# MoBA scores on halves of the TensorE array: each head's products on its own 64 rows, each head into its own PSUM bank

## The chip, the cores and the metric

The kernel runs on one NeuronCore of a Trainium2 chip. The metric is the device time of one execution in microseconds (us). TensorE (PE) multiplies, VectorE (DVE) and ScalarE (ACT) read its results from PSUM and do the elementwise work, GpSimd (POOL) works on SBUF only, and SyncE (SP) issues the DMAs. All engines run beside each other and wait for one another by semaphores; each works off its own instructions in the order in which the program lists them.

## The reference, cut to what matters

The program is a decoder trunk of four layers over 256 tokens of width 1024. Layers 0 and 3 mix tokens by native sparse attention (NSA), layer 1 by MoBA, layer 2 by a short convolution; each layer ends with a SwiGLU feed-forward part. The change is in the one MoBA layer. With 256 tokens there is one MoBA block, so no past block is selected and the layer is plain causal attention with 16 heads of width 64:

```python
q, k, v = jnp.split(h @ w_in, 3, axis=-1)
q = heads(q) * (HEAD_DIM ** -0.5)
k = heads(k); v = heads(v)
m_own = own_pos[None, :] <= tq[:, None]
s_own = jnp.einsum('bhqd,bhkd->bhqk', qc, k_own)
p = masked_softmax(s_own, m_own)
o = jnp.einsum('bhqk,bhkd->bhqd', p.astype(v_own.dtype), v_own)
return o @ w_out
```

## The kernel before, in words

All large products are made from float32 values that are split into a high part (rounded to float32r, the format in which TensorE takes them in one instruction) and a low part (the rest). A product of two such values is three matmuls: high by high, high by low, low by high. Weights come from memory in parts of 128 x 1024; the high part is a CAST on ACT or DVE (line 109) and the low part a subtraction on DVE or POOL (line 110). Five buffers hold the high parts and five the low parts (`W_BUFS`), so the CAST of a later part can only start when TensorE is done with the part that had the buffer.

In the MoBA layer two heads are worked on together, as a pair: there are eight pairs, called p0 to p7 here. `MOBA_ORDER` lists the steps of the layer: `V` values, `k` a projection of the keys of one pair, `q` a projection of its queries, `s` its scores and softmax, `T` the transposes of its probabilities, `P` their product with the values. A projection is 24 matmuls (lines 128 to 130) into one PSUM bank of the pool "A"; DVE then scales the result (line 324), and ACT and DVE split it (lines 166 and 167 for queries, 379 and 380 for keys). The pool "A" has four banks, "B" three and "C" one. They are handed out in turn: who asks for a fifth bank of "A" waits until the last reader of the first one is done.

The two heads of a pair lie in the 128 partitions: head 0 in partitions 0 to 63, head 1 in 64 to 127. The keys are kept in a tile `keys` of 128 partitions with one half for each head, and the 64 partitions that belong to the other head hold zeros (`pad_keys`). So `scores` (line 412) can use all 128 partitions: for the first 128 tokens (t = 0) three matmuls of 256 columns (two heads by 128 keys) fill one bank, and for the other 128 tokens (t = 1) three matmuls of 512 columns (two heads by 256 keys) fill another. Half of what is multiplied is zero.

`softmax` (line 345) then does, for each of four blocks (t = 0 head 0, t = 0 head 1, t = 1 head 0, t = 1 head 1), one instruction on DVE that adds the mask and takes the row's extreme (line 354, with a second short instruction that reads the extreme out), one exponential on ACT (line 357), and after a reciprocal of the four sums on DVE (line 359) one multiplication on POOL (line 361). `turn` transposes the result on TensorE into banks of "B" (lines 431 to 434) and splits it into tiles `pt` (lines 166 and 167); `weigh` multiplies by the values into the bank of "C" and splits the outcome (lines 453 and 454).

The program's instructions are written in the order of the steps, and a scheduler at build time then sets the order on each engine; it knows nothing of the measured times. So an edit of one step can move instructions of others.

Of the kernel before, what the change touches and what calls it, by code (L numbers as in the profile page):

```python
# [16 lines left out]
P = 128  # L17
D = 1024
S = 256
# [4 lines left out]
DH = 64  # L24
# [27 lines left out]
class Kernel:  # L52
# [334 lines left out]
    def moba(self, norm):  # L387
        nc, at = self.nc, self.begin(norm)
        mm = nc.tensor.matmul
# [21 lines left out]

        def scores(p):
            q, kt = qs[p], self.keys[p % 4]
            s = []
            for t in range(NT):
                n = (t + 1) * P
                o = self.bank("A")[:, :2 * n].rearrange("p (a s) -> p a s", a=2)
                c = slice(t * P, (t + 1) * P)
                mm(o, q[:, 0, c], kt[:, 0, :, :n], start=True, stop=False)
                mm(o, q[:, 1, c], kt[:, 0, :, :n], start=False, stop=False)  # L420
                mm(o, q[:, 0, c], kt[:, 1, :, :n], start=False, stop=True)
                s.append(o)
            cols = [(s[t][:, i], slice((t + i) * S if t else i * P, (t + i + 1) * S if t else (i + 1) * P))
                    for t in range(NT) for i in range(2)]
            prs.append(self.softmax(cols, [1.0] * 4))

# [14 lines left out]
        def weigh(p):  # L441
# [8 lines left out]
            for i in range(2):  # L450
# [5 lines left out]

        self.steps(MOBA_ORDER, {"V": lambda _: self.values(at, put_values), "k": project_k, "q": project_q,
                                "s": scores, "T": turn, "P": weigh})
        self.out_proj(outs, norm + 1)

# [483 lines left out]
```

## Time and profile before

| | |
|---|---|
| median of three runs | 1308.08 us (1306.71 to 1308.45) |
| the profiled execution | 1307.79 us |
| its span, from the first to the last instruction | 1306.0 us |
| busy in the span: PE / DVE / ACT / POOL | 1259.8 / 985.9 / 715.6 / 319.9 us |
| mean granted clock of TensorE | 0.993 |
| the chain of work that ended last, by engine | PE 84%, DVE 9%, the rest 2% or less each |
| the MoBA scores | eight pairs, first matmul at 402.2 us, last at 456.7 us |

The span is what the trace covers; the 1.8 us around it belong to the execution too. Busy time of PE counts an instruction until its result has left the array, so instructions overlap in the trace: how fast PE works is read from the distance of their starts, not from their durations.

### The profile page before, as it was taken

To read this page: it belongs to the slowest core of one execution; us is meant where nothing else is said; L and a number is where in the kernel's file an instruction comes from. 1 tells how busy PE (TensorE), PEld (TensorE's weight loads), DVE (VectorE), ACT (ScalarE), POOL (GpSimd) and SP (SyncE) were. 2 spreads that over 40 slices of the span, in tenths; PEclk is the share of its full clock that TensorE was granted. 3 is DMA by queue.
4 is the path that set the end of the run, shared out by engine and by line. 5 is a ranking of instruction groups with operands and counts; after the bars stand their busy time and mean duration, and the time that the engine had idled before them with its cause. 6 is when DMAs were issued, how large, how long until landed. Compare 5 with 4: busy or idle time off the path is not lost.

```text
span 1306.0 us, 21378 instructions
## 1 busy us (share of the span) xinstructions
PE 1259.8 (96%) x7820; PEld 1122.1 (86%) x7820; DVE 985.9 (75%) x1939; ACT 715.6 (55%) x1443; POOL 319.9 (24%) x346
## 2 busy tenths in 40 slices
PE   6988999999999899999999999999998989999997
PEld 6977788888889888888899988888898878888886
DVE  6688899775778888876667789765767797997753
ACT  3468857564434546655433447564324797666532
POOL 5557620000247220000113120000244765000011
PEclk9999999999999999999999999999999999999999
DMA  6623065656554335755565655656555312565551
GB/s 231 244 86 102 17 208 163 209 184 197 185 172 149 100 114 179 212 189 194 165 201 170 200 179 171 201 186 195 189 179 193 98 49 66 193 210 187 187 179 60
DMA packets 60728, 215.24 MB, mean 165 GB/s; under 512 B 7248, under 2 KB 7632, under 8 KB 60624
## 3 DMA queue, kind: packets, MB, share of 16 engines
q1 hardware_dynamic: 60480, 213.85, 50.5%
q8 instruction: 61, 1.00, 0.3%
q14 instruction: 43, 0.35, 0.1%
q10 hardware_dynamic: 144, 0.04, 0.0%
HBM read 212.81 MB, written 1.05 MB: 164 GB/s over the span
## 4 chain that ended last, share of the span: by engine, by line
PE 84%; DVE 9%; ACT 2%; issue 2%; POOL 2%; DMA 1%; POOLq 0%; DVEq 0%; ACTq 0%
PE psA L148 30%; PE psA L152 15%; PE psB L148 11%; PE psB L152 5%; PE psA L130 4%; PE psA L128 4%; PE psA L129 4%; PE psB L549 2%; DVE pt L167 1%; DVE pr L354 1%; ACT pr L357 1%; DVE ff L167 1%; PE psA L337 1%; POOL wlo L110 1%; DVE wlo L110 1%
## 5 line engine op out<-in xcount | busy, mean ns | idle before, releaser
L109 ACT CAST whi<-raw 128x1024 fp32r<-128x1024 f32 (+1 forms) x354 | 369.0, 1043 | 297.4 <-PE psB L148 110.6
L110 DVE TENSOR_TENSOR wlo<-raw,whi 128x1024 fp32r<-128x1024 f32 (+1 forms) x334 | 412.4, 1238 | 140.1 <-ACT whi L109 134.9
L148 PE MATMUL psA<-ff,whi 128*128 128x512 f32 x840 | 231.2, 396 | 0.2
L148 PEld LDWEIGHTS psA<-ff,whi 128*128 128x128 f32 x840 | 149.0, 188 | 25.1 <-DVE ff L167 0.6
L195 POOL TENSOR_TENSOR ssq<-ssq,row 128x256 f32<-128x256 f32 x54 | 50.7, 938 | 483.4 <-issue 291.5
L148 PE MATMUL psA<-pt,whi 128*128 128x512 f32 x640 | 166.4, 395 | 0.0
L128 PE MATMUL psA<-at,whi 128*128 128x256 f32 x552 | 160.5, 291 | 5.9 <-ACT whi L109 5.9
L130 PE MATMUL psA<-at,wlo 128*128 128x256 f32 x552 | 159.0, 289 | 3.8 <-DVE wlo L110 3.8
L129 PE MATMUL psA<-at,whi 128*128 128x256 f32 x552 | 159.1, 288 | 0.0
L110 POOL TENSOR_TENSOR wlo<-raw,whi 128x1024 fp32r<-128x1024 f32 (+1 forms) x56 | 132.4, 2370 | 82.1 <-ACT whi L109 52.5
L148 PEld LDWEIGHTS psA<-pt,whi 128*128 128x128 f32 x640 | 116.5, 188 | 21.2
L152 PEld LDWEIGHTS psA<-ff,wlo 128*128 128x128 f32 x840 | 122.8, 188 | 12.4
L152 PE MATMUL psA<-ff,wlo 128*128 128x256 f32 x840 | 129.2, 281 | 0.0
L128 PEld LDWEIGHTS psA<-at,whi 128*128 128x128 f32 x552 | 108.5, 197 | 6.2 <-ACT whi L109 5.9
L130 PEld LDWEIGHTS psA<-at,wlo 128*128 128x128 f32 x552 | 108.2, 196 | 4.4 <-DVE wlo L110 4.4
L129 PEld LDWEIGHTS psA<-at,whi 128*128 128x128 f32 x552 | 108.6, 197 | 0.5
L152 PEld LDWEIGHTS psA<-pt,wlo 128*128 128x128 f32 x640 | 87.1, 188 | 7.3
L152 PE MATMUL psA<-pt,wlo 128*128 128x256 f32 x640 | 88.9, 281 | 0.0
L148 PE MATMUL psB<-pt,whi 128*128 128x512 f32 x320 | 84.8, 395 | 0.0
L361 POOL TENSOR_SCALAR pr<-pr,rc,gates 128x256 f32<-128x256 f32 (+1 forms) x128 | 70.3, 563 | 38.6 <-DVE rc L359 32.5
L357 ACT ACTIVATE pr<-pr,mn 128x128 f32<-128x128 f32 (+1 forms) x160 | 71.3, 449 | 9.5 <-DVE mn L354 8.7
L292 ACT ACTIVATE row<-gu 128x256 f32<-128x256 f32 x88 | 36.8, 418 | 67.9 <-DVE gu L284 61.2
(207 smaller groups left out, 2210.6 us busy)
## 6 DMA issues: line engine op xcount, KB each, us to landing
raw<-in_w SPq DMA_DIRECT2D x384, 512.0 KB, 4.0
wf<-in_w SPq DMA_DIRECT2D x16, 512.0 KB, 4.4
h<-in_xt SPq DMA_DIRECT2D x4, 256.0 KB, 5.4
raw<-in_w SPq DMA_DIRECT2D x4, 256.0 KB, 5.4
out<-ff SPq DMA_DIRECT2D x4, 256.0 KB, 2.5
w<-in_w SPq DMA_DIRECT2D x2, 256.0 KB, 3.8
mask<-in_mask SPq DMA_DIRECT2D x1, 128.0 KB, 6.6
cneg<-in_cneg SPq DMA_DIRECT2D x1, 128.0 KB, 6.3
```

The costliest lines, as they stand in the source:

```text
L109: copy(hi[:, c], src[:, c])
L110: eng.tensor_tensor(out=lo[:, c], in0=src[:, c], in1=hi[:, c].bitcast(F32), op=OP.subtract)
L128: mm(out, wt[0], act[0], start=first, stop=False)
L129: mm(out, wt[0], act[1], start=False, stop=False)
L130: mm(out, wt[1], act[0], start=False, stop=last)
L148: mm(outs[o], w[0], acts[k].rearrange("p i s -> p (i s)"), start=(k == 0), stop=(k == n - 1))
L152: mm(outs[o][:, :S], w[1], acts[k][:, 0, :], start=False, stop=False)
L167: self.nc.vector.tensor_tensor(out=dst[:, 1], in0=src, in1=dst[:, 0].bitcast(F32), op=OP.subtract)
L195: nc.gpsimd.tensor_tensor(out=self.ssq, in0=self.ssq, in1=sq, op=OP.add)
L292: nc.scalar.activation(sg, gu[:, 0, :], AF.Silu)
L357: nc.scalar.activation(pr[:, c], pr[:, c], AF.Exp, bias=mn[:, j:j + 1], scale=-1.0, accum_out=den[:, j:j + 1])
L361: nc.gpsimd.tensor_scalar(pr[:, c], pr[:, c], rc[:, j:j + 1], gates[j], op0=OP.mult, op1=OP.mult)
```

## The change

`scores` takes its two banks at the start, one for each head instead of one for each half of the tokens. Each matmul takes 64 partitions of queries and keys (those of one head), and the two heads alternate. Per pair there are twelve matmuls in place of six: for t = 0 six of 128 columns, for t = 1 six of 256 columns. Columns 0 to 127 of a bank hold t = 0, columns 128 to 383 hold t = 1. The softmax reads the same four blocks at their new places. The zeros in `keys` are still written, but MoBA no longer reads them. All lines behind `scores` move up by two (454 is 452 now).

```diff
         def scores(p):
             q, kt = qs[p], self.keys[p % 4]
-            s = []
+            s = [self.bank("A") for _ in range(2)]
             for t in range(NT):
-                n = (t + 1) * P
-                o = self.bank("A")[:, :2 * n].rearrange("p (a s) -> p a s", a=2)
-                c = slice(t * P, (t + 1) * P)
-                mm(o, q[:, 0, c], kt[:, 0, :, :n], start=True, stop=False)
-                mm(o, q[:, 1, c], kt[:, 0, :, :n], start=False, stop=False)
-                mm(o, q[:, 0, c], kt[:, 1, :, :n], start=False, stop=True)
-                s.append(o)
-            cols = [(s[t][:, i], slice((t + i) * S if t else i * P, (t + i + 1) * S if t else (i + 1) * P))
+                n, c = (t + 1) * P, slice(t * P, (t + 1) * P)
+                for m, (a, b) in enumerate(((0, 0), (1, 0), (0, 1))):
+                    for i in range(2):
+                        r = slice(i * DH, (i + 1) * DH)
+                        mm(s[i][:, t * P:t * P + n], q[r, a, c], kt[r, b, i, :n], start=(m == 0), stop=(m == 2))
+            cols = [(s[i][:, t * P:2 * t * P + P], slice((t + i) * S if t else i * P, (t + i + 1) * S if t else (i + 1) * P))
                     for t in range(NT) for i in range(2)]
             prs.append(self.softmax(cols, [1.0] * 4))
```

The order of instructions moves at several places. The first is on PE, from the scores of p1 to the projection behind them (`keys1` and `ff_498` are keys and queries of p1, `psA_511` and `psA_512` its banks, `psA_518` the bank of the next projection, `whi117` its weights). Before:

```order
L419 MATMUL psA_511_4483<-keys1_104,ff_498_4348 128x256 [waits DVE_49,Activation_49]
L420 MATMUL psA_511_4483<-keys1_104,ff_498_4348 128x256
L421 MATMUL psA_511_4483<-keys1_104,ff_498_4348 128x256
L419 MATMUL psA_512_4487<-keys1_104,ff_498_4348 128x512 [waits DVE_49]
L420 MATMUL psA_512_4487<-keys1_104,ff_498_4348 128x512
L421 MATMUL psA_512_4487<-keys1_104,ff_498_4348 128x512
L128 MATMUL psA_518_4509<-at_454_3752,whi117_4316 128x256 [waits DVE_49,PE_49]
```

Now, from the second matmul of p1 on:

```order
L420 MATMUL psA_512_4490<-keys1_104,ff_498_4348 128x128 [waits DVE_49]
L420 MATMUL psA_511_4489<-keys1_104,ff_498_4348 128x128
L420 MATMUL psA_512_4490<-keys1_104,ff_498_4348 128x128
L420 MATMUL psA_511_4489<-keys1_104,ff_498_4348 128x128
L420 MATMUL psA_512_4490<-keys1_104,ff_498_4348 128x128
L420 MATMUL psA_511_4489<-keys1_104,ff_498_4348 128x256
L420 MATMUL psA_512_4490<-keys1_104,ff_498_4348 128x256
L420 MATMUL psA_511_4489<-keys1_104,ff_498_4348 128x256
L420 MATMUL psA_512_4490<-keys1_104,ff_498_4348 128x256
L420 MATMUL psA_511_4489<-keys1_104,ff_498_4348 128x256
L420 MATMUL psA_512_4490<-keys1_104,ff_498_4348 128x256
L128 MATMUL psA_518_4521<-at_454_3752,whi117_4316 128x256 [waits DVE_49]
```

Both banks of p1 are wanted at the first two matmuls; before, the second one was wanted at the fourth matmul. `psA_518` is the fifth bank after `psA_505`, the first bank of p0, and takes its place.

The second place is on DVE, at the scaling of the last key projection ahead of p0's softmax (`row_504`; `psA_505` and `psA_506` are the banks of p0, `wlo121` the low half of a weight part, `keys3` the keys of p3). Before:

```order
L109 CAST whi121_4512<-raw121_4510 128x1024 [waits DMAHW0_49,PE_49]
L324 TENSOR_TENSOR row_504_4452<-psA_503_4421,rb_485_4181 128x256 [waits PE_49]
L354 ISA pr_507_4466,mn_508_4467<-psA_505_4458,mask_84 128x128 [waits PE_49]
L354 ISA mn_508_4467 128x1
L354 ISA pr_507_4466,mn_508_4467<-psA_505_4458,mask_84 128x128
L354 ISA mn_508_4467 128x1
L380 TENSOR_TENSOR keys3_106<-row_504_4452,keys3_106 64x256 [waits Activation_49] x2
L354 ISA pr_507_4466,mn_508_4467<-psA_506_4462,mask_84 128x256 [waits PE_49]
L354 ISA mn_508_4467 128x1
```

Now:

```order
L109 CAST whi121_4524<-raw121_4522 128x1024 [waits DMAHW0_49,PE_49]
L324 TENSOR_TENSOR row_504_4452<-psA_503_4421,rb_485_4181 128x256 [waits PE_49]
L110 TENSOR_TENSOR wlo121_4525<-raw121_4522,whi121_4524 128x1024 [waits DVE_49]
L380 TENSOR_TENSOR keys3_106<-row_504_4452,keys3_106 64x256 [waits Activation_49] x2
L354 ISA pr_507_4472,mn_508_4473<-psA_505_4458,mask_84 128x128 [waits PE_49]
L354 ISA mn_508_4473 128x1
L354 ISA pr_507_4472,mn_508_4473<-psA_506_4459,mask_84 128x128 [waits PE_49]
L354 ISA mn_508_4473 128x1
L354 ISA pr_507_4472,mn_508_4473<-psA_505_4458,mask_84 128x256
```

The subtraction of `wlo121` and the two of `keys3` stand ahead of p0's four blocks now; `wlo121` stood behind p1's blocks before. The bank `psA_505` had its last reader in the second block; now it has it in the third, since each bank holds t = 0 and t = 1 of one head. The first block waits for all of its bank's matmuls, t = 1 among them.

The third place is on DVE too, at the softmax of p3 (`pr_540`, `rc_543`), which is followed by the split of p1's transposed probabilities (`pt_548`). Before, from the last block but one of p3:

```order
L354 ISA pr_540_4700,mn_541_4701<-psA_539_4696,mask_84 128x256 [waits PE_49]
L354 ISA mn_541_4701 128x1
L354 ISA pr_540_4700,mn_541_4701<-psA_539_4696,mask_84 128x256
L354 ISA mn_541_4701 128x1
L454 TENSOR_TENSOR ff_545_4724<-psC_544_4717,ff_545_4724 64x256 [waits Activation_49]
L110 TENSOR_TENSOR wlo125_4747<-raw125_4744,whi125_4746 128x1024
L359 RECIPROCAL rc_543_4703<-den_542_4702 128x4 [waits Activation_49,Pool_49]
L454 TENSOR_TENSOR ff_545_4724<-psC_544_4717,ff_545_4724 64x256 [waits Activation_49]
L167 TENSOR_TENSOR pt_548_4737<-psB_546_4729,pt_548_4737 128x512 [waits Activation_49]
```

Now, from the instruction behind the scaling `row_537`:

```order
L110 TENSOR_TENSOR wlo125_4771<-raw125_4768,whi125_4770 128x1024 [waits DVE_49]
L167 TENSOR_TENSOR ff_535_4674<-row_537_4706,ff_535_4674 128x256 [waits Activation_49]
L354 ISA pr_540_4724,mn_541_4725<-psA_538_4710,mask_84 128x128 [waits PE_49]
L354 ISA mn_541_4725 128x1
L354 ISA pr_540_4724,mn_541_4725<-psA_539_4711,mask_84 128x128 [waits PE_49]
L354 ISA mn_541_4725 128x1
L354 ISA pr_540_4724,mn_541_4725<-psA_538_4710,mask_84 128x256
L354 ISA mn_541_4725 128x1
L354 ISA pr_540_4724,mn_541_4725<-psA_539_4711,mask_84 128x256
L354 ISA mn_541_4725 128x1
L359 RECIPROCAL rc_543_4727<-den_542_4726 128x4 [waits Activation_49,Pool_49]
L452 TENSOR_TENSOR ff_545_4748<-psC_544_4741,ff_545_4748 64x256 [waits Activation_49]
```

The subtraction of `wlo125` moved from behind the four blocks to ahead of them, the reciprocal `rc_543` stands right behind the blocks, and `pt_548` comes next in the list as before; on ACT the first cast of `ff_545`, which stood between the exponentials of p3, now stands behind all four. At the pairs p4 to p7 the pattern repeats: a subtraction of a weight part stands ahead of the blocks of p5 (`wlo130`), and before the reciprocal of p5 there is now a CAST of a weight part (`whi131`).

## Rows read from the trace of the kernel before

**Rows 1.** Page, parts 1 and 5: PE of the whole span; all exponentials of line 357.

```profile
PE 1259.8 (96%) x7820; PEld 1122.1 (86%) x7820; DVE 985.9 (75%) x1939; ACT 715.6 (55%) x1443; POOL 319.9 (24%) x346
...
L357 ACT ACTIVATE pr<-pr,mn 128x128 f32<-128x128 f32 (+1 forms) x160 | 71.3, 449 | 9.5 <-DVE mn L354 8.7
```

**Rows 2.** Windows: stretch of the MoBA scores; busy us by engine, then PEclk, DMA share.

```profile
400.00:466.00 66.00, 60.09 (x422) 54.97 (x422) 56.32 (x148) 37.44 (x116) 30.47 (x39) 0.97 0.33 106
```

**Rows 3.** Timeline of PE (start us, us, instruction): scores of p3, next product.

```profile
419.39 0.28 PE L419 MATMUL psA<-keys,ff 128*128 128x256 f32 x1
...
419.74 0.40 PE L419 MATMUL psA<-keys,ff 128*128 128x512 f32 x1
...
420.45 0.39 PE L128 MATMUL psC<-pt,ff 128*128 128x512 f32 x1
```

**Rows 4.** Timeline of PE: eight matmuls of one column, then a projection.

```profile
24.37 0.28 PE L213 MATMUL psB<-ones,ssq 128*128 128x1 f32 x2
...
25.18 0.36 PE L128 MATMUL psA<-at,whi 128*128 128x256 f32 x1
```

**Rows 5.** Timeline of PE: float32 products of 128 columns, two instructions each.

```profile
82.46 1.15 PE L593 MATMUL psB<-w,row 128*128 128x128 f32 x8
83.36 0.36 PE L129 MATMUL psA<-at,whi 128*128 128x256 f32 x1
```

**Rows 6.** Timeline of PE: p0, p1 and the next projection.

```profile
403.03 0.40 PE L421 MATMUL psA<-keys,ff 128*128 128x512 f32 x1
...
405.38 0.50 PE L419 MATMUL psA<-keys,ff 128*128 128x512 f32 x1 [1.60 <-DVE row L324]
...
406.18 0.28 PE L128 MATMUL psA<-at,whi 128*128 128x256 f32 x1
```

**Rows 7.** Timeline of DVE: the softmax of p0 and p1 begins.

```profile
404.90 0.42 DVE L324 TENSOR_TENSOR row<-psA,rb 128x256 f32<-128x256 f32 x1
405.24 0.28 DVE L354 CUSTOM_DVE_ANT_0 pr<-psA,mask 128x128 f32<-128x128 f32 x1
...
405.44 0.29 DVE L354 CUSTOM_DVE_ANT_0 pr<-psA,mask 128x128 f32<-128x128 f32 x1
...
405.79 0.87 DVE L380 TENSOR_TENSOR keys<-row,keys 64x256 fp32r<-64x256 f32 x2
406.69 0.42 DVE L354 CUSTOM_DVE_ANT_0 pr<-psA,mask 128x256 f32<-128x256 f32 x1
...
408.50 1.22 DVE L110 TENSOR_TENSOR wlo<-raw,whi 128x1024 fp32r<-128x1024 f32 x1
```

**Rows 8.** Timeline of DVE: from a CAST of weights to the split of `pt_548`.

```profile
416.65 2.64 DVE L109 CAST whi<-raw 128x1024 fp32r<-128x1024 f32 x1
...
419.30 0.39 DVE L324 TENSOR_TENSOR row<-psA,rb 128x256 f32<-128x256 f32 x1
420.22 2.40 DVE L380 TENSOR_TENSOR keys<-row,keys 64x256 fp32r<-64x256 f32 x2 [0.53 <-ACT keys L379]
422.65 0.76 DVE L109 CAST whi<-raw 128x1024 fp32r<-128x1024 f32 x1
...
423.66 0.27 DVE L354 CUSTOM_DVE_ANT_0 pr<-psA,mask 128x128 f32<-128x128 f32 x1
...
427.38 1.02 DVE L167 TENSOR_TENSOR pt<-psB,pt 128x512 fp32r<-128x512 f32 x2
```

**Rows 9.** Timeline of PE: last transpose before a wait, and after it.

```profile
425.14 0.27 PE L433 MATMUL psB<-ident,pr 128*128 128x128 f32 x1
428.12 0.33 PE L434 MATMUL psB<-ident,pr 128*128 128x128 f32 x1 [2.71 <-DVE pt L167]
```

**Rows 10.** Windows of 1 us behind that wait; the column behind POOL is PEclk.

```profile
428.00:429.00 1.00, 0.88 (x6) 0.79 (x7) 1.00 (x4) 0.67 (x2) 0.60 (x2) 0.84 0.76 254
429.00:430.00 1.00, 1.00 (x4) 0.81 (x3) 1.00 (x2) 0.95 (x3) 0.00 (x0) 0.50 0.53 213
...
432.00:433.00 1.00, 1.00 (x10) 1.00 (x10) 0.01 (x1) 0.37 (x1) 0.00 (x0) 0.95 0.49 197
```

## Prediction

> **What bounds the kernel now.** I read the busy shares first, then the chain of waits, then the stretch of the MoBA scores alone. Over the whole span PE is busy 96% of the time [rows 1], and the chain that ended last runs through PE for most of its length: a microsecond that PE loses or saves is one of the kernel, except where PE itself waits. So the question is where PE waits near the scores. From 400 to 466 us it is busy 60.09 of 66 us and DVE 56.32 [rows 2]: two engines that are both nearly full and take turns in being late. The timeline of PE shows two long waits there: 1.60 us inside p1's scores, for a bank of pool A that DVE has not read out yet [rows 6], and 2.71 us in the transposes of p2, for a bank of pool B, which the split of `pt_548` on DVE frees [rows 9]. Behind the second, the granted clock falls to 0.50 (1.2 GHz): 0.84 in the first microsecond, 0.50 in the next three (the first of them is shown), 0.95 in the one after [rows 10]. In full-speed time this lost 0.16 + 3 x 0.50 + 0.05 = 1.7 us. Behind the wait of 1.60 us it did not fall: three matmuls of 512 columns take 0.80 us there [rows 6], the 0.71 of p3 [rows 3] and a little for the start.
>
> **The price of the products.** Before, the scores of p3 take from 419.39 to the next product at 420.45: 1.06 us, of which 0.35 for three matmuls of 256 columns (0.12 each) and 0.71 for three of 512 (0.24 each) [rows 3]. Eight pairs are 8.5 us. After the change a pair is six matmuls of 128 columns and six of 256, each with a weight load of its own. No float32r product of under 256 columns and none on 64 rows stands in this trace, so I bound its price by neighbours. Eight matmuls of a single column, where streaming costs nothing, start 0.81 / 8 = 0.10 us apart [rows 4]: a weight load and its matmul do not go faster than this when they follow each other on the full array. Float32 products of 128 columns cost 0.90 / 8 = 0.11 us per instruction, and they take two instructions each, so 0.225 per product [rows 5].
>
> - One after the other at 0.11: 6 x 0.11 + 6 x 0.12 = 1.38 us per pair, 0.32 more than now, 2.6 us over eight pairs.
> - Two heads at a time, weight loads too: 3 x 0.11 + 3 x 0.12 = 0.69 us, 0.37 less, 3.0 us saved over eight pairs.
> - One after the other, with the narrow ones at the float32 price: 6 x 0.225 + 6 x 0.12 = 2.07 us, 1.01 more, 8.1 us over eight pairs.
>
> I take the first. Its 0.11 lies on the row that is nearest in shape and in the number of instructions, and all matmuls of this trace stand one behind the other. The other two are the ends of the range.
>
> The Trainium skill speaks for the second: "TensorE: Matmul & The Clock Gate", section "Part 3: Packing small matmuls", says that products on different row strips of the array run at the same time, and gives 3.07 times the speed for four strips of 32 rows. No run here shows two products at once. By that rule alone the sum for the products would be the saving of the second line.
>
> **What moves with it, p0 and p1.** The order puts two things ahead of p0's softmax on DVE: the subtraction of `wlo121` and the two of `keys3`. The scaling ahead of them starts at 404.90 and takes 0.42; `wlo121` takes about 1.2 (the same instruction at 408.50), `keys3` 0.87, the blocks of 128 columns 0.20 each by their starts, one of 256 about 0.4 [rows 7]. The third block then ends at 404.90 + 0.42 + 1.2 + 0.87 + 0.2 + 0.2 + 0.4 = 408.2. It is the last reader of `psA_505`, and the projection `psA_518` behind p1 needs that bank. Before, the second block was the last reader, over by 405.7, and the projection began at 406.18 without a wait [rows 6]. Now PE waits until about 408.2: **2.0 us later**. The twelve products of p1 start at 405.38, as soon as their second bank is free, and even at 2.07 us they end by 407.5: inside this wait their price does not count, nor does p0's.
>
> **Up to the wait for `pt_548`.** PE has 2.71 us in hand there [rows 9]. The 2.0 us and 0.32 each for p2 and p3 make 2.6 and would just vanish, if DVE came at its old time. It does not. The CAST of weights that began at 416.65 [rows 8] needs a weight buffer that PE frees at the end of the first projection behind p2, so it begins 2.0 + 0.32 = 2.3 us later. It took 2.64 where the one at 422.65 took 0.76. If it now takes 0.76, the scaling that started at 419.30 starts at 419.7, 0.4 late; if it keeps its stretch, 2.3 late. POOL's list now has p2's multiplications ahead of its next subtraction, so less of POOL's work should stand beside the CAST: I take 0.6, and 2.3 as the bound. The stretched `keys` step at 420.22 (2.40 against 0.87 in [rows 7]) I leave as it is. From the first block of p3 at 423.66 to `pt_548` at 427.38 it took 3.7 us [rows 8]. Now it is: 1.2 for `wlo125`, 0.35 for the query split, 0.2 for the first block, about 0.2 until ACT starts, four exponentials at 0.449 [rows 1] (1.8), which the reciprocal now waits for with nothing of DVE's in between, and then 0.2 for it, and 0.7 for the first split of `ff_545` and its cast on ACT: 4.6. So `pt_548` comes 0.6 + 0.9 = **1.5 us later**, and this stands in place of the 2.0 above, not beside it.
>
> PE's wait shrinks to 2.71 + 1.5 - 2.6 = 1.6 us. That is the length of the wait at 405.38, behind which the clock stayed, and far under the 2.71 behind which it fell. I take it that the clock stays at 2.4 GHz: **1.7 us back**.
>
> **p4 to p7.** PE is nearly without waits from here on, and so is DVE. Four pairs at 0.32 are 1.3 us; I put half of it on the path, 0.6, for the other half runs while DVE is late anyway. In the softmax of p5, `wlo130` (1.2) moves ahead of the blocks and the CAST of `whi131` (0.76) ahead of the reciprocal, where `wlo130` stood: the probabilities come about 0.8 later, and PE waits for them in the transposes: **0.8**. No DMA is added or moved, and POOL's and ACT's work is the same.
>
> **Sum.** 1.5 - 1.7 + 0.6 + 0.8 = +1.2 us on the profiled execution, 1307.79 us (span 1306.0 and 1.8 around it), which lies 0.3 under the median of the runs: 1309.0 us. What can be told from no change is about 0.2%, 2.6 us. So the forecast is no difference that can be measured, with a lean to slower; its own range is 1306 to 1311.5, the upper end with the clock falling as before (+1.7) and the scores of p4 to p7 wholly on the path; the bound of the CAST (1.7 more, and the clock's fall with it) lies above it, in the wide range.
>
> **Rivals.**
>
> 1. *The halves run together.* For it: the two heads share no row and no bank. Against it: each product loads weights of its own, and 0.10 us between starts even for one column [rows 4] says that loads count. At 0.69 us a pair p0 and p1 still end inside the wait at the bank. p2 to p7 save 6 x 0.37 = 2.2 on PE; with DVE's turns about half reaches the end, -1.1 instead of +0.6. By the sum: 1.5 - 1.7 - 1.1 + 0.8 = -0.5, 1307.3 us; where also DVE's 1.5 at `pt_548` does not come true, 1305. Faster than 1305.5 only in that second half.
> 2. *Narrow products at the float32 price*, on the other side. For it: every float32r product here has at least 256 columns, so nothing says that 128 are cheap; the one product of 128 columns that is not a transpose costs 0.225 [rows 5]. Against it: those are two instructions, these one. p2 and p3 take 2.0 more and, with the 2.0 at the bank, use up the 2.71 us; p4 to p7 take 4.0 more, of which I put 3.3 on the path, since PE becomes the later engine. About 2.0 + 2.0 - 2.7 = 1.3 at `pt_548` falls under DVE's 1.5. Sum: 1.5 - 1.7 + 3.3 + 0.8 = +3.9, and with 1.7 if the clock falls +5.6: 1311.7 to 1313.4. It decides from about 0.17 us per narrow product.
> 3. *A switch between whole array and halves empties the array.* A matmul of 256 columns takes 0.28 us and the next starts 0.12 later [rows 3]: 0.16 are in flight, and would be waited for. The new order has 18 switches (p0 and p1 in one visit, p6 in three, since transposes stand among its products), so 18 x 0.16 = 2.9 us on PE; four of them hide at the two waits, and of the rest some 2.0 reach the end: 1311.0 us.
>
> The Trainium skill, "TensorEngine Tiling (Array Packing)", section "Key Properties", states that changing the tiling mode drains TensorE. No row here shows such a change, so it has a chance of its own as rival 3.
>
> 4. *The change does nothing that can be seen*, with the clock's fall unchanged and DVE absorbing all: 1308. This lies inside the forecast.
>
> **How the numbers follow.** Forecast (with rival 4) 0.50, rival 1 0.18, rival 2 0.20, rival 3 0.12. Faster by over 0.2% (under 1305.5): 0.10 from rival 1 and 0.03 from the forecast's low end. Slower by over 0.2% (above 1310.7): 0.18 from rival 2, 0.07 from rival 3 and 0.10 from the forecast's high end, where the clock falls. The rest, 0.52, is within. The range of eight in ten reaches from 1304.8, in rival 1, to 1314, at the top of rival 2.
>
> **What will show it.** Right or wrong can be read from: the distance of starts in the scores (0.11 and 0.12; pairs of starts close together mean rival 1; over 0.2 for 128 columns rival 2; a gap at the first product of each visit rival 3); a wait of 1 to 2 us on PE behind p1 for a block of line 354; the wait at the transposes of p2, and the granted clock behind it; the start of the reciprocal of p3 behind its exponentials. The forecast fails if the wait behind p1 adds to the one at p2 instead of using it up, or if the clock falls at a new place.

## The result, and the profile after

The changed kernel takes 1319.18 us (median of 4 runs, 1315.82 to 1321.37); the kernel before took 1307.39 beside it (4 runs, 1306.01 to 1308.45). The ratio is 1.0082, 95% interval 1.0065 to 1.0100: slower, by 11 to 12 us, outside the predicted range. The profiled execution took 1318.85 us, its span is 1317.1, 11.1 more than before.

PE's busy time and the whole span hardly tell why. The first line is the page's part 1, the second the line of the exponentials, [rows 1]; the third is the window that answers to [rows 2]. The exponentials now wait 16.2 us in all, 9.5 before.

```profile
PE 1263.9 (96%) x7868; PEld 1124.9 (85%) x7868; DVE 985.6 (75%) x1939; ACT 715.4 (54%) x1443; POOL 319.8 (24%) x346
...
L357 ACT ACTIVATE pr<-pr,mn 128x128 f32<-128x128 f32 (+1 forms) x160 | 71.2, 448 | 16.2 <-DVE mn L354 12.7
```

```profile
400.00:466.00 66.00, 55.07 (x422) 51.15 (x420) 50.55 (x124) 30.84 (x93) 27.89 (x31) 0.90 0.35 112
```

In 400 to 466 us PE is busy 55.07 us and no longer 60.09, DVE 50.55 and no longer 56.32, and the mean clock is 0.90 instead of 0.97. Work of the same size has been spread over a longer time: both engines wait more, for each other and for POOL. The list of PE's waits from 400 to 480 us (us in total, times, the longest) shows for whom:

```profile
PE psB L429 <- POOL pr L361: 3.4, 2, 3.1
PE psB L432 <- DVE pt L167: 2.7, 1, 2.7
PE psA L420 <- DVE row L324: 2.1, 1, 2.1
PE psA L128 <- DVE mn L354: 1.8, 1, 1.8
```

The second and the third were there before (2.71 in [rows 9], 1.60 in [rows 6]). The last is new, and the first was short: its long part, 3.1 us, was 0.52 before (shown below).

**The wait behind p1.** PE, timeline; then DVE in the same stretch:

```profile
404.32 1.01 PE L420 MATMUL psA<-keys,ff 64*128 64x128 f32 x13
407.38 0.95 PE L420 MATMUL psA<-keys,ff 64*128 64x128 f32 x11 [2.05 <-DVE row L324]
410.18 0.58 PE L128 MATMUL psA<-at,whi 128*128 128x256 f32 x1 [1.85 <-DVE mn L354]
```

```profile
406.91 0.42 DVE L324 TENSOR_TENSOR row<-psA,rb 128x256 f32<-128x256 f32 x1
407.24 1.22 DVE L110 TENSOR_TENSOR wlo<-raw,whi 128x1024 fp32r<-128x1024 f32 x1
408.38 0.86 DVE L380 TENSOR_TENSOR keys<-row,keys 64x256 fp32r<-64x256 f32 x2
409.27 0.29 DVE L354 CUSTOM_DVE_ANT_0 pr<-psA,mask 128x128 f32<-128x128 f32 x1
...
415.54 0.69 DVE L109 CAST whi<-raw 128x1024 fp32r<-128x1024 f32 x1 [3.86 <-PE psA L129]
```

The blocks of p0 stand behind `wlo121` and `keys3`, as the order had it, and the projection waits 1.85 us for the third of them. The granted clock falls there, at a place where it had stayed (windows of 1 us, the column behind POOL is PEclk):

```profile
408.00:409.00 1.00, 0.33 (x5) 0.13 (x3) 0.97 (x3) 0.98 (x2) 0.00 (x0) 0.80 0.22 70
409.00:410.00 1.00, 0.00 (x0) 0.00 (x0) 0.97 (x6) 0.89 (x3) 0.00 (x0) 0.50 0.51 98
...
415.00:416.00 1.00, 1.00 (x9) 1.00 (x8) 0.46 (x1) 0.00 (x0) 0.00 (x0) 0.79 0.00 0
```

The projections run at 1.2 GHz to 415 us, and now DVE waits for PE: 3.86 us for the weight buffer that the CAST at 415.54 needs, which the first projection behind p1 frees when it ends.

**The wait for `pt_548`** did not shrink. PE's row answers to [rows 9], the windows to [rows 10]:

```profile
434.52 0.33 PE L432 MATMUL psB<-ident,pr 128*128 128x128 f32 x1 [2.67 <-DVE pt L167]
```

```profile
435.00:436.00 1.00, 1.00 (x7) 0.87 (x6) 1.00 (x3) 0.72 (x2) 0.01 (x1) 0.95 0.00 0
436.00:437.00 1.00, 1.00 (x7) 1.00 (x6) 1.00 (x2) 0.95 (x3) 0.00 (x0) 0.50 0.00 0
```

It stands 6.4 us later (428.12 to 434.52), and so does what lies ahead of it on PE: p3's products start 6.5 us later (419.39 to 425.89).

**The wait in p5's transposes.** PE and POOL before:

```profile
452.70 0.33 PE L431 MATMUL psB<-ident,pr 128*128 128x128 f32 x1 [0.52 <-POOL pr L361]
```

```profile
452.27 2.03 POOL L361 TENSOR_SCALAR pr<-pr,rc 128x128 f32<-128x128 f32 x4 [11.10 <-DVE rc L359]
454.99 2.42 POOL L110 TENSOR_TENSOR wlo<-raw,whi 128x1024 fp32r<-128x1024 f32 x1 [0.68 <-PE psB L434]
```

PE, POOL and DVE after:

```profile
459.33 0.80 PE L420 MATMUL psA<-keys,ff 64*128 64x128 f32 x9 [0.91 <-ACT pr L357]
463.19 0.47 PE L429 MATMUL psB<-ident,pr 128*128 128x128 f32 x1 [3.06 <-POOL pr L361]
```

```profile
460.27 2.34 POOL L110 TENSOR_TENSOR wlo<-raw,whi 128x1024 fp32r<-128x1024 f32 x1 [11.97 <-issue]
462.60 1.95 POOL L361 TENSOR_SCALAR pr<-pr,rc 128x128 f32<-128x128 f32 x4
```

```profile
456.30 1.22 DVE L110 TENSOR_TENSOR wlo<-raw,whi 128x1024 fp32r<-128x1024 f32 x1
...
459.44 0.69 DVE L109 CAST whi<-raw 128x1024 fp32r<-128x1024 f32 x1
460.62 0.18 DVE L359 RECIPROCAL rc<-den 128x4 f32<-128x4 f32 x1 [0.48 <-ACT pr L357]
```

The CAST of `whi131`, now ahead of the reciprocal, lets POOL start `wlo131` at 460.27; p5's multiplications stand behind it and begin at 462.60, though their reciprocal was over at 460.8. Before, POOL had them ahead: the multiplications at 452.27, the subtraction at 454.99. The clock is at 0.50 from 464 to 470 us.

A ledger of the stage, from the starts of PE's instructions in the two timelines, us: A is from p0's first product to p4's, B from there to p5's first transposes, C from there to the last row of p7's, "rest" from there to the end of the span; "clock" is the full-speed time that the granted clock took away from 400 to 484 us, as the sum of 2 x (1 - PEclk) over windows of 2 us.

```
                     p0 starts    A      B      C    A+B+C  rest   clock
before                 402.2     31.9   18.6   10.5   61.0  842.8   1.7
after                  404.3     36.3   22.6   11.7   70.6  842.2   8.5
```

The whole difference of 11.1 us is A +4.4, B +4.0, C +1.2, 2.1 by which the stage starts later, and -0.6 behind it. That start lies ahead of all that was changed (before p0 the traces of the two kernels list the same instructions in the same order on all four engines) and scatters: from 401.7 to 405.2 us in the kernels below.

### The profile page after: what moved, and what is told of

Same layout as the page of the kernel before. It is cut to its first block, busy times and chain, and to the rows that moved or that the text cites. A ratio compares the mean times of both kernels' runs of the same rounds, so it can differ in the third digit from the quotient of the medians.

```text
span 1317.1 us, 21473 instructions
## 1 busy us (share of the span) xinstructions
PE 1263.9 (96%) x7868; PEld 1124.9 (85%) x7868; DVE 985.6 (75%) x1939; ACT 715.4 (54%) x1443; POOL 319.8 (24%) x346
## 4 chain that ended last, share of the span: by engine, by line
PE 84%; DVE 8%; ACT 3%; issue 2%; POOL 2%; DMA 1%; POOLq 0%; DVEq 0%; ACTq 0%
PE psA L148 30%; PE psA L152 15%; PE psB L148 11%; PE psB L152 5%; PE psA L128 4%; PE psA L130 4%; PE psA L129 4%; PE psB L547 2%; ACT pr L357 1%; POOL wlo L110 1%; DVE pt L167 1%; DVE wlo L110 1%; DVE whi L109 1%; DVE pr L354 1%; PE psC L708 1%
## 5 line engine op out<-in xcount | busy, mean ns | idle before, releaser
L128 PEld LDWEIGHTS psA<-at,whi 128*128 128x128 f32 x552 | 109.9, 199 | 8.8 <-ACT whi L109 6.1
L129 PEld LDWEIGHTS psA<-at,whi 128*128 128x128 f32 x552 | 109.9, 199 | 0.4
L357 ACT ACTIVATE pr<-pr,mn 128x128 f32<-128x128 f32 (+1 forms) x160 | 71.2, 448 | 16.2 <-DVE mn L354 12.7
```

What stands on the lines that cost most here:

```text
L128: mm(out, wt[0], act[0], start=first, stop=False)
L129: mm(out, wt[0], act[1], start=False, stop=False)
L357: nc.scalar.activation(pr[:, c], pr[:, c], AF.Exp, bias=mn[:, j:j + 1], scale=-1.0, accum_out=den[:, j:j + 1])
```

## The experiments

Theory A: the order that came with the change makes the new waits; the products are cheaper. Theory B: the half products, their loads or the switches cost the time. Theory C: the two banks by head are enough by themselves. D and E, on the clock, come with the seventh run. The old order is that of the kernel before, the new order that of the changed kernel. Each run has one trace, of one execution, while its time is a median; the traced execution took 1308.34 us in run 1, and 1319.85, 1319.37, 1314.21 and 1321.75 us in runs 5, 6, 10 and 12, so times and stages agree only to 1 to 4 us there.

The order can be pinned: a table lists, for an engine, the numbers of its instructions as the program text issues them, and each instruction is tied behind its forerunner in the table (an edge of order alone, without a wait).

```diff
+    def pin(self):
+        ...
+        for e, order in ORDER.items():
+            for x, y in zip(order, order[1:]):
+                self.tc.add_manual_dep(at[e][y], at[e][x].name, mybir.DependencyInfo(
+                    mybir.DependencyClass.NoSync, mybir.DependencyReason.DATA), reason="pin")
```

With it, lines of the stage lie 8 further down in the traces, those of the transposes 10 to 22.

**1. Half products, old order.** The changed kernel and the table of the order before, for all four engines.

> The changed products and banks, with the instructions of DVE, ACT, POOL and PE (other than the products) pinned to the order of the kernel before; nothing of the computation is left out. Theory A (the order that came with the change makes the new waits of PE behind p1 and in the transposes of p5, and the clock falls behind them; the products themselves are cheaper, 0.73 to 0.9 us a pair against 1.06): both waits shrink to under 1 us, 1305 to 1309 us. Theory B (the half-array products, their weight loads or the switches to and from them cost the time): it stays at 1316 to 1320. Theory C (two banks by head, of which the older is read out a block later, are enough by themselves): the wait behind p1 stays over 1 us, that in p5 goes, 1311 to 1315.

Measured 1310.55 us (10 runs, 1308.34 to 1312.48), ratio to before 1.0016 (1.0007 to 1.0025). The two new waits are all but gone:

```profile
406.54 0.58 PE L136 MATMUL psA<-at,whi 128*128 128x256 f32 x1 [0.29 <-DVE mn L362]
452.22 0.33 PE L439 MATMUL psB<-ident,pr 128*128 128x128 f32 x1 [0.68 <-POOL pr L369]
```

So 8.6 of the 11 to 12 us are the order. B and C fall as causes of the bulk. A's range is missed by 1.5 us; what is left above before is small.

**2. Full products, banks by head.**

```diff
-                        mm(s[i][:, t * P:t * P + n], q[r, a, c], kt[r, b, i, :n], start=(m == 0), stop=(m == 2))
+                        mm(s[i][:, t * P:t * P + n], q[:, a, c], kt[:, b, i, :n], start=(m == 0), stop=(m == 2))
```

> The changed kernel with products over all 128 rows again (the other head's rows of the keys are zero): banks by head, and on every engine the same order as the changed kernel; only the operands of the 96 products differ. Theory A: as slow as the changed kernel or a little slower, since a pair's twelve products now follow each other at 0.11 us, 1.3 us against 0.8, part of it under waits: 1318 to 1322 us. Theory B: the loss goes, 1307 to 1310. Theory C: 1317 to 1321, which does not tell it from A.

Measured 1319.08 us (4 runs, 1318.66 to 1320.15), ratio to before 1.0081 (1.0064 to 1.0098). The halves are neither the loss nor a gain: without them the time is that of the changed kernel to 0.1 us. The order of this kernel is the same as the changed one's on every engine, so it is the banks by head (and the twelve products they ask for) that the scheduler answers with another order, not the halves. What this kernel does show is their price. p3's products here, and in the changed kernel, each with the row behind them:

```profile
424.26 1.54 PE L420 MATMUL psA<-keys,ff 128*128 128x128 f32 x12
425.64 0.39 PE L128 MATMUL psC<-pt,ff 128*128 128x512 f32 x1
```

```profile
425.69 0.28 PE L130 MATMUL psA<-at,wlo 128*128 128x256 f32 x1
425.89 0.95 PE L420 MATMUL psA<-keys,ff 64*128 64x128 f32 x12
426.78 0.50 PE L128 MATMUL psC<-pt,ff 128*128 128x512 f32 x1
```

Twelve full products take 1.38 us, exactly 6 x 0.11 + 6 x 0.12. Twelve halves take 0.89: two at a time, with a little lost at the ends (0.20 from the last matmul to the first half, where 0.12 is usual).

**3. Full products, banks by head, old order.** The edit of 2 with the table of 1.

> Full products, banks by head, and the order of the kernel before pinned as in the first run of this set. Theory A: near the kernel before, 1307 to 1311 us (twelve products at 0.11 us make a pair 0.3 us longer than six). Theory B: 1307 to 1310. Theory C: 1311 to 1316, with a wait of over 1 us behind p1. The difference to the first run is what the half products are worth by themselves: A expects them 0.5 to 3 us faster, B 6 to 10 us slower.

Measured 1309.80 us (10 runs, 1308.15 to 1310.51), ratio to before 1.0009 (0.9999 to 1.0018). Banks by head cost about 1.4 us where the order is kept, with an interval of -0.1 to 2.4. Beside run 1 the halves are not faster but 0.75 us slower, inside the scatter: A's 0.5 to 3 us of gain did not come.

**4. Old products and banks, new order.** The kernel before with the table of the changed one.

> The kernel before (six products a pair, banks by half of the tokens) with the instructions of DVE, ACT, POOL and PE pinned to the order of the changed kernel (the products of p6 in one visit, not three); nothing of the computation is left out. Theory A: the wait in p5's transposes (3 us, with the clock behind it) is there, and DVE's lateness at p0 too, but the bank of p0's first half is free after its second block: 1312 to 1319 us. Theory B and theory C: 1306 to 1310.

Measured 1315.51 us (4 runs, 1314.49 to 1317.58), ratio 1.0053 (1.0038 to 1.0068). The order alone costs 7 us in the kernel that has nothing else of the change. Its wait in p5's transposes is as long as the changed kernel's (PE's waits, 400 to 480 us):

```profile
PE psB L441 <- POOL pr L369: 3.3, 1, 3.3
PE psB L444 <- DVE pt L175: 2.6, 1, 2.6
```

The same order with the banks by head (run 2, +10.7) is 3.6 us dearer. Here the clock does not fall behind p1, and A is 33.7 where it is 36.0 in run 2 (the table below).

**5. POOL's step alone.** In the changed kernel's own table, `wlo131` (POOL's 179) stands behind p5's multiplications (167 to 170).

```diff
-    "Pool": "104 106-114 123-129 131 130 132-146 151 147-150 156 152-155 157-161 166 162-165 179 167-178 180-186 193 195 187-192 194 196-197 200 198-199 203 201-202 206 204-205 209 207-208 212 210",
+    "Pool": "104 106-114 123-129 131 130 132-146 151 147-150 156 152-155 157-161 166 162-165 167-170 179 171-178 180-186 193 195 187-192 194 196-197 200 198-199 203 201-202 206 204-205 209 207-208 212 210",
```

> The changed kernel, its order on DVE, ACT and PE kept, with one step moved: POOL's subtraction wlo131 stands behind p5's multiplications again, as before. Nothing is left out. Theory A (order): the wait of 3.06 us in p5's transposes goes down by about the 2.34 us of that subtraction, and with it the clock's fall at 463 to 470 us (3.4 us in full-speed time): 4 to 6 us less than the changed kernel, 1313 to 1315 us. Rival: DVE, which is also late there (its subtraction wlo130 and the CAST of whi131 stand ahead of p5's and p6's softmax), makes the same wait again: 1317 to 1319.

Measured 1317.82 us (4 runs, 1317.24 to 1319.85): the rival's range. The wait went from 3.06 to 1.5 us and B from 22.6 to 20.7, but C rose from 11.7 to 13.3, and the clock stayed low longer (5.1 us lost from 460 to 472, against 3.4). Whether DVE or the clock took the gain back, this run does not tell.

**6. DVE at p0 and p1 alone.** The changed kernel's table, DVE's 42 instructions there in the old order.

> The changed kernel, with only DVE's order of the stretch of p0 and p1 (the 42 instructions up to the CAST behind p1's softmax) put back to that of the kernel before: p0's blocks ahead of wlo121 and keys3. The rest of the order, on every engine, is the changed kernel's. Theory A: the wait of 1.85 us for p0's older bank goes down to about 1, as in the run with the whole old order, and the clock's fall behind it gets shorter: 2 to 4 us less, 1315 to 1317 us. Rival: the wait of 2.7 us for pt_548 further on takes back what is saved: 1318 to 1320.

Measured 1315.87 us (4 runs, 1314.36 to 1319.37): inside A's range, at 3.3 us under the changed kernel. A goes from 36.3 to 34.0; the wait behind p1 from 1.85 to 0.8. The wait at `pt_548` took back little of it (2.67 to 2.3).

**7. The waits filled.** The changed kernel in its own order, with products that nobody reads.

```diff
+            if p < 2:
+                fill(self.bank("C"), p, 12)
...
+        def fill(o, p, n):
+            return [mm(o[:, :S], qs[p][:, 0, :P], self.keys[p % 4][:, 0, 0, :], start=True, stop=True)
+                    for _ in range(n)]
...
+            if p == 5:
+                self.fills = fill(b0, p, 20)
```

> The changed kernel in its own order, with extra products on PE whose results nobody reads: 12 of 256 columns behind p0's products, 12 behind p1's (1.44 us each), 20 ahead of p5's transposes (2.4 us). The waits stay as long, but PE works in them. Theory D (it is the clock's fall behind the waits that costs most): the clock stays at 1.00 behind p1 and behind p5's transposes, 2.7 + 3.4 us come back: 1312 to 1315 us. Theory E (the waits cost, and the slower clock runs beside DVE's work): 1317 to 1321.

Measured 1316.50 us (4 runs, 1315.30 to 1317.62), between D and E. The clock does what was wanted: 1.00 behind p1 and behind p5's transposes, 1.7 us lost in the stage instead of 8.5.

```profile
408.00:410.00 2.00, 1.82 (x15) 1.82 (x16) 1.69 (x13) 2.00 (x11) 0.21 (x1) 1.00 0.53 201
410.00:412.00 2.00, 2.00 (x19) 2.00 (x19) 0.71 (x2) 1.23 (x6) 1.42 (x4) 1.00 0.00 0
```

```profile
464.00:466.00 2.00, 0.62 (x4) 0.43 (x4) 1.72 (x8) 1.49 (x8) 1.52 (x4) 1.00 0.00 0
```

But of 6.8 us of full-speed time the kernel got 2.7 back. A fell from 36.3 to 33.8: by these two traces the clock's fall behind p1 cost 2.5. Runs 5 and 13 below bear this out: up to p4 they have the changed kernel's order and its wait of 1.85 us, the clock's fall behind it took 1.7 us in place of 3.4, and A is 35.5 and 35.4. B and C stayed (22.6 each, 11.6 against 11.7): behind p5's transposes PE at full clock is busy 0.62 of the 2 us in the last row and waits for the others. There the slow clock cost nothing that these traces show.

**8. Blocks head by head, half products, old order.**

```diff
-                    for t in range(NT) for i in range(2)]
+                    for i in range(2) for t in range(NT)]
```

> The changed products and banks in the order of the kernel before (as the first run of the first set, 1310.55 us), with the softmax's blocks head by head (both halves of head 0, then both of head 1), so that the older bank is read out after the second block and not the third. Nothing is left out. Theory C (the bank by head costs what is left over the kernel before): the wait behind p1, 1.2 us there, goes down by the 0.4 us of a block, and 1 to 2 us come back: 1308 to 1309.5 us. Rival (what is left is the clock's fall behind the wait of 2.0 us inside p1's scores, which starts from two banks at once): no difference, 1310 to 1311.

Measured 1308.01 us (10 runs, 1306.14 to 1312.84), ratio to before 1.0006 (0.9993 to 1.0019): the size that C asked for, but its reason was misread from run 1. The 1.2 us there is not behind p1 (0.29 us, the row under 1); it is in the output projection, at 457.95 us, for a bank of the last scores. Both waits are gone here, and A is 30.6 where it was 32.0.

**9 and 10. Half of the order back.** The changed kernel, pinned to the old order from p4's softmax on (9), or for p0 to p3 (10).

> The changed kernel with the order of DVE, ACT, POOL and PE put back to that of the kernel before from p4's softmax on; p0 to p3 keep the changed kernel's order. Nothing is left out. From the traces so far, p4's first product to p5's first transposes takes 18.6 us before, 22.6 in every kernel with the whole new order, 20.7 with POOL's step alone put back, which then lost 1.7 of its 1.9 us by the end of p7's transposes. If DVE's steps there (wlo130 ahead of p5's blocks, the CAST of whi131 ahead of p5's reciprocal) are what POOL's step alone did not cure, all 4 us come back: 1314 to 1316 us. Rival (PE arrives late from p0 to p3 and the rest only follows): 1317 to 1320.

> The other half: p0 to p3 in the order of the kernel before, p4 to p7 in that of the changed kernel. Nothing is left out. In the traces the stretch from p0's first product to p4's takes 31.9 us before, 36.3 in the changed kernel, 32.0 with the whole old order, 34.0 with p0 and p1 alone put back. If the two halves simply add, 4 us come back here and the wait in p5's transposes stays: 1314 to 1316 us, and the two gains of this pair of runs make the 8.6 us between the changed kernel and the run with the whole old order. If the first half's gain only lets PE wait longer at p5's transposes: 1317 to 1320.

Measured 1315.04 us (4 runs, 1313.87 to 1315.27) and 1313.16 (6 runs, 1312.06 to 1314.21). They are 4.1 and 6.0 us under the changed kernel, together 10.1 where the whole old order gave 8.6: the halves add, as far as the scatter tells. In 9 the wait in p5's transposes is 1.6 us, in 10 it is the old 3 (PE's waits, 400 to 480 us, one row of each):

```profile
PE psB L441 <- POOL pr L369: 1.6, 1, 1.6
```

```profile
PE psB L441 <- POOL pr L369: 3.0, 1, 3.0
```

In 10 the clock falls behind p1 for as long as in the changed kernel (3.4 us lost from 406 to 416 in either), and A is 32.1 all the same: with the old order of p0 to p3, what PE loses there is made up by p4, since the wait at `pt_548` shrinks to 0.94 us.

**11. The candidate.** Run 8 with the fill of run 7 behind p0 (12) and p1 (6).

> The candidate against both kernels: half products, blocks head by head, the old order (as the run of 1308.01 us), with 12 extra products of 256 columns behind p0's scores and 6 behind p1's, whose results nobody reads. If the fall of the clock behind p1 (1.7 us in full-speed time in that run) costs its length, 1306 to 1307 us; if DVE sets the pace in this stage, the time that PE gains there is waited again at pt_548, and the time stays at 1307.5 to 1309 us. Chance of the second 0.7: in the run of the changed kernel with its waits filled 6.8 us of full-speed time came back and 2.7 us of the kernel's.

Measured 1308.27 us (11 runs, 1305.94 to 1310.17), ratio to before 0.9996 (0.9985 to 1.0006). The clock never falls from 400 to 484 us, and it is worth nothing: at `pt_548` PE waits 1.7 us, where run 8 has 1.2. Nothing found here beats the kernel before.

**12 and 13. Two parts of the second half.** From p4 on, DVE's and POOL's order back together (12), PE's alone (13), the rest as in the changed kernel.

> The changed kernel in its own order, with DVE's and POOL's order put back to the old one from p4's softmax on; ACT's and PE's stay. Nothing is left out. If the loss of the second half is POOL's step and DVE's steps together (theory A), the whole gain of the run with all four engines put back comes: 1314 to 1316 us, and p4's first product to p5's first transposes falls from 22.6 to about 19.6. Rival (PE's order there, with the transposes of p3 and p5 at other places among the products and projections): as POOL's step alone, 1317 to 1319.

> The changed kernel in its own order, with PE's order alone put back to the old one from p4's scores on. Nothing is left out. Theory A: no change, 1318 to 1320.5 us, since the probabilities of p5 come no earlier. Rival (PE's order): 1314 to 1316.

Measured 1320.58 us (4 runs, 1320.08 to 1321.75), ratio 1.0090 (1.0070 to 1.0110), and 1326.51 (4 runs, 1325.26 to 1329.20), ratio 1.0139 (1.0119 to 1.0160). Neither came as any theory said. In 12 the stretch that A named does what it said (B 19.7), and all of it is lost behind: PE, in its new order, now waits at the next pair's transposes. Its waits there in 12, and then in 13:

```profile
459.96 0.33 PE L441 MATMUL psB<-ident,pr 128*128 128x128 f32 x1 [1.62 <-POOL pr L369]
...
468.57 0.47 PE L441 MATMUL psB<-ident,pr 128*128 128x128 f32 x1 [4.12 <-POOL pr L369]
```

```profile
461.60 0.47 PE L441 MATMUL psB<-ident,pr 128*128 128x128 f32 x1 [3.05 <-POOL pr L369]
...
475.71 0.33 PE L441 MATMUL psB<-ident,pr 128*128 128x128 f32 x1 [2.36 <-POOL pr L369]
```

In 13 the wait in p5's transposes stays as long as in the changed kernel, and one in p7's comes on top. The four queues fit each other: the old order of all (run 9) is 4.1 us under the changed kernel, parts of it are 1.4 and 7.3 us over.

All stages in one table (us, as above; the runs' medians behind it):

```
                     p0 starts    A      B      C    A+B+C  rest   clock  median
before                 402.2     31.9   18.6   10.5   61.0  842.8   1.7   1307.3 to 1308.4
after                  404.3     36.3   22.6   11.7   70.6  842.2   8.5   1319.2
 1 halves, old order   401.7     32.0   18.5   12.1   62.6  842.2   3.4   1310.6
 2 full, by head       402.7     36.0   22.7   11.8   70.4  843.8   8.5   1319.1
 3 as 2, old order     403.7     30.8   18.7   12.3   61.8  842.9   1.7   1309.8
 4 before, new order   403.6     33.7   22.7   10.7   67.0  843.9   5.1   1315.5
 5 POOL's step         404.7     35.5   20.7   13.3   69.5  843.8   8.5   1317.8
 6 DVE at p0, p1       405.2     34.0   22.6   11.9   68.5  844.0   8.5   1315.9
 7 waits filled        402.3     33.8   22.6   11.6   68.0  843.6   1.7   1316.5
 8 head by head, old   402.6     30.6   18.3   12.0   60.9  841.0   3.4   1308.0
 9 second half back    403.8     36.0   19.7   12.1   67.8  841.6   6.8   1315.0
10 first half back     404.0     32.1   21.4   10.8   64.3  844.1   5.1   1313.2
11 8 and fill          402.5     30.3   18.3   12.0   60.6  842.7   0.0   1308.3
12 DVE, POOL from p4   404.0     36.3   19.7   15.3   71.2  844.6   8.5   1320.6
13 PE from p4          403.6     35.4   22.6   16.7   74.7  845.9  10.2   1326.5
```

Read it by columns. B is 18.3 to 19.7 wherever DVE and POOL have the old order from p4 on, 21.4 to 22.7 where they have the new one, 20.7 with POOL's step alone; products, banks and PE's order do not move it. C takes it back where PE's order does not go with theirs. A follows the first half's order, and in the new order the clock adds to it: A is 33.7 and 33.8 where the clock stays behind p1 (runs 4 and 7), 34.0 with DVE's old order there (run 6), and 35.4 to 36.3 otherwise. Run 4 has the old banks and run 7 the banks by head, so as far as these two tell, the banks show in A only by way of the clock. A+B+C puts the runs in the order of their medians, but for neighbours whose medians lie within 0.7 us. The column of the clock does not.

## Why the prediction was wrong

**The price of the products** was taken at 1.38 us a pair. That is the price of twelve full products (run 2, to the hundredth); the halves cost 0.89, rival 1's mechanism. The Trainium skill ("TensorE: Matmul & The Clock Gate", "Part 3: Packing small matmuls") says that products on different row strips run at the same time; the traces agree, 0.89 us in place of 1.38. But neither value reaches the end: runs 1 and 3, and the changed kernel and run 2, differ by 0.75 and 0.1 us. The half that the sum put on the path (+0.6) was too much for either. Rivals 2 and 3 fall: there are no 0.225 us products, and a switch costs about 0.08 us, not 0.16 (0.20 against 0.12 at p3's entry). One sum of rival 1 is off: without DVE's 1.5 its 1307.3 becomes 1305.8 and not 1305.

**p0 and p1: right.** The wait of 2.0 us was 1.85, at the instruction and for the block that were named, and the projection came 1.9 us later relative to p0's start (1.85 after p1's products, 4.0 later in all, 2.1 of it the stage's start).

**`pt_548`: here the prediction failed.** It said that DVE's 1.5 us would stand in place of PE's lateness, since PE had 2.71 in hand. The 1.5 were 0.6 by which DVE comes late to p3's softmax, and 0.9 for the longer way from there. DVE's rows (their forerunners are in [rows 8]):

```profile
423.61 0.69 DVE L109 CAST whi<-raw 128x1024 fp32r<-128x1024 f32 x1
...
426.26 2.78 DVE L109 CAST whi<-raw 128x1024 fp32r<-128x1024 f32 x1
...
429.30 1.21 DVE L110 TENSOR_TENSOR wlo<-raw,whi 128x1024 fp32r<-128x1024 f32 x1
...
433.11 0.18 DVE L359 RECIPROCAL rc<-den 128x4 f32<-128x4 f32 x1 [1.16 <-ACT pr L357]
...
433.77 0.69 DVE L167 TENSOR_TENSOR pt<-psB,pt 128x512 fp32r<-128x512 f32 x1
```

The 0.9 were right: from `wlo125` at 429.30 to `pt_548` at 433.77 it takes 4.5 us, 4.6 were said, and the reciprocal waits for ACT with nothing of DVE's in between. The 0.6 were 3.5: what follows the scaling starts at 429.30, before at 423.66, less the 2.1 of the stage's start. The prediction had let PE's lateness reach DVE through one CAST's weight buffer, 2.3 us late, and counted on most of it being won back, since that CAST would lose its stretch. It did (0.69), but the next one was stretched instead (2.78). And PE's lateness had reached DVE before, at the CAST of 415.54: that starts 3.4 us late by the same count, behind a projection that itself came 1.9 late and ran at 1.2 GHz. So `pt_548` came 4.3 us late and not 1.5, and PE came to it 4.3 late (transpose ahead of it at 431.58, before at 425.14) and not 2.6. What PE lost went through DVE into the very thing PE then waits for: the slack of 2.71 us was not PE's to spend. The wait stayed 2.67, the clock fell there as before, and the forecast's gain of 1.7 did not come.

**The clock.** The prediction took it that the clock stays behind p1, since it had stayed behind 1.60 us. It fell, 0.80 at 408 to 0.79 at 415 us, and run 7 puts its price in A at 2.5 us. The 1.9 of the wait and these 2.5 make up the +4.4 of A. The prediction named a fall at a new place as what would make it fail, and gave it no term.

**p5: a term missed.** The 0.8 us for DVE's steps was 4.0 in B; PE's wait there alone grew from 0.52 to 3.06. "POOL's and ACT's work is the same" is true of the work and false of its order: a subtraction of 2.34 us came ahead of the multiplications that PE waits for. Run 5 moved that step alone and got 1.9 us of B back, run 12 with DVE's steps 2.9; both lost it in C, and only run 9, with PE's and ACT's order too, kept 4.1 of the median. So the prediction's term was too small, and the way it was made could not have found it: it priced steps one engine at a time, and what the order costs is how the four queues stand to each other.

**What the loss is.** Of 11 to 12 us, 8.6 are the order (run 1 against the changed kernel; 7.1 by run 4, which has nothing else of the change), about 1.4 the banks by head where the order is old (run 3, interval -0.1 to 2.4), and the halves nothing that can be told. The kernel's time follows the order; the products, which the change is about, do not show in it. That PE waits again for what it gains in this stage, as in run 11, is the likely reason, and argued rather than shown. Still open: why run 1 stays 2.1 us above before (its trace, of an execution of 1308.34 us, cannot say), where run 8, with the same products, is at 0.7 with an interval that takes in zero; and why the clock fell behind p1 in runs 1, 3 and 8 (below).

## What to carry to other kernels

Where a scheduler sets the order, a change of who owns a bank is a change of the order on every engine: list what moved on each of them, POOL's queue too, before costing the operation that the diff is about. Slack at a wait can be spent only if what ends the wait does not itself depend on the late engine. And a faster product need not show in a stage where PE waits for the other engines; pinning the whole old order around the new operations tells the two apart in a single run, while pinning one engine's part can be worse than either order.

## What the hardware showed that was not expected

- Half products of two heads start in pairs: the twelve of p3 start from 425.89 to 426.57 us, and the next instruction at 426.78, 0.89 us behind the first; twelve full ones need 1.38.
- The granted clock fell in or behind p1's products in runs 1, 3 and 8, after waits of 2.04, 1.54 and 2.04 us, but not in the kernel before (1.60) nor in run 4, whose trace has 1.58 and 1.58:

```profile
406.80 0.96 PE L420 MATMUL psA<-keys,ff 128*128 128x512 f32 x3 [1.58 <-DVE row L332]
409.35 0.36 PE L136 MATMUL psA<-at,whi 128*128 128x256 f32 x1 [1.58 <-DVE mn L362]
```

  The length of the waits does not sort these. Without fills, the kernels where the clock stayed have six long products in p0 and p1, those where it fell have twelve short ones; that this is the reason was not tried. Nor does one wait fix how long the fall lasts: behind the same 1.85 us it took 3.4 us of full-speed time in the changed kernel and 1.7 in runs 5 and 13.
- 3.4 us of full-speed time lost at 1.2 GHz behind p5's transposes cost nothing that the traces show (run 7): PE at full clock waited for the others there.
